# Attention's q and z in pairs of tiles, by seven block products in a stage of their own

## The chip, the core and the metric

The kernel runs on one core of a Trainium2 chip. The metric is the device time of one execution in microseconds; three runs of the kernel before took 3054.83 to 3066.11 us, median 3056.27. PE is the matrix engine (TensorE), DVE VectorE, ACT ScalarE, POOL GpSimd and SP SyncE, which here issues most DMAs.

## What is computed

One layer of a hybrid encoder, for 512 prompt and 64 sample tokens (T = 576) of width 2048:

```python
h = rmsnorm(x, norm_w) * (1.0 + scale[:, None]) + shift[:, None]
proj = h @ w_in          # q|k|v and z, beta, a of DeltaNet; q, k, v, z of attention; indexer; two gates
o_a = gated_delta_rule(l2norm(qa), l2norm(ka), va, g, beta, S0)        # after conv4 and silu
y_a = (rmsnorm(o_a, gdn_norm_w) * silu(z_a)) @ w_branch_a
o_b = sparse_attention(q_b, q_i, w_i, q_pos, K, V, KI, topk, rel_bias) # top-k keys by the indexer's score
y_b = (o_b * jax.nn.silu(z_b)) @ w_branch_b
merged = jax.nn.sigmoid(gl_a) * y_a + jax.nn.sigmoid(gl_b) * y_b
x = x + gate[:, None] * (merged @ w_out)
```

All is fp32. Attention has 16 heads of 128 over two groups of keys and values, DeltaNet 16 heads of 128.

## The kernel before

The projections are a stream of tiles (`plan`). A tile is 128 columns of a weight matrix, all 2048 rows in 16 blocks, times all 576 tokens in two halves of 288. Activations and weights are split into a high part (rounded fp32r) and a low part, and three products are summed (high x high, high x low, low x high), so a tile is 16 x 3 x 2 = 96 matmuls of 288 columns. `load` fetches the raw tile on SP's queue three tiles ahead; `split` makes its parts while the tile before runs: two ACT copies for each of four quarters, and an accumulating DMA from POOL's queue that turns the negated high part into the low part. Each tile ends in an epilogue (`..._epi`) that reads PSUM, and may begin with a `pre`.

All else (indexer scores, top-k, DeltaNet, attention, the ada-gate sums, loads of later stages) is written as generator tasks. After every matmul `tick` (L156) steps the tasks that are due by a cost model of the engines; so the order of all instructions is fixed at build time. `join` (L165) holds the stream until tasks are done and lets tasks alone be issued meanwhile; `drain` joins all tasks. Tiles have few buffers, and `wait`, `take` and `room` make a task wait for their users.

The order of the stream before: k (2 tiles), misc (indexer key, beta, a), 8 indexer q tiles, v (2), a gate tile, `open_gdn` (L1763, drains all but top-k), 6 gate tiles, 16 DeltaNet heads (three conv tiles, then a z tile or gate tile, a few more gate tiles), 3 gate tiles, `open_att` (L1775, drains), 16 pairs of a q and a z tile with 2 gate tiles, 4 z tiles of DeltaNet, `open_ga` (L1786, drains), 8 gate tiles beside `load_ga` (L1558), `open_branch` (drains), then the w_branch_a, w_branch_b and w_out tiles, 16 each.

Attention: `bias_setup` (L1278) writes each head's bias row 128 times to DRAM (3 MB, d_F) at `open_att`. `kv_load` (L1319) fetches a group's keys and values. Per head `qb_epi` copies q out of PSUM and `zb_epi` (L1477) makes silu(z) and spawns `attend` (L1340): it loads the bias tile BT, then four prompt blocks (`attend_block`), each with one logit buffer L; after an odd head `attend_sample` (L1393) does the sample tokens of the pair of heads and stores gb to d_gb. The pres join earlier heads, since qT has two buffers, gb three and zt four. `gate_vectors` (L1510) sums the ada gate on DVE from 64 loads of 256 KB, with a gap of 5000 between them. DeltaNet's `decays` and `solve` of head h wait for the scan of head h-2; `solve` stores N to DRAM (dN), and loads its solved blocks back (TT, Df).

Of the kernel before, what the change touches and what calls it, by code (L numbers as in the profile page):

```python
# [16 lines left out]
D = 2048  # L17
KO = 16
# [190 lines left out]
class Kern(Plan):  # L209
# [53 lines left out]

    def load(self, n):
        if n >= len(self.stream):
            return
        d = self.stream[n]
        m = d["m"] = sum(w for _, _, w in d["srcs"])
        raw = d["raw"] = self.wp.tile([128, 2048], F32, tag="wraw", name=f"wraw{n}")
        r3 = raw[:, :KO * m].rearrange("p (k m) -> p k m", m=m)  # L270
        at = 0
        for src, c, w in d["srcs"]:
            self.S.dma_start(r3[:, :, at:at + w], src[:, c:c + w].rearrange("(k p) m -> p k m", p=128))
            at += w

    def split(self, n, q, of=4, eng=None):
        if n >= len(self.stream):
            return
        d = self.stream[n]
        if q == 0:  # L280
            d["hi"] = self.wp.tile([128, 2048], F32R, tag="whi", name=f"whi{n}")
            d["lo"] = self.wp.tile([128, 2048], F32R, tag="wlo", name=f"wlo{n}")
        w = KO * d["m"] // of
        s = slice(w * q, w * q + w)
        self.A.activation(d["hi"][:, s], d["raw"][:, s], AF.Copy)
        if eng:
            eng.tensor_tensor(d["lo"][:, s], d["raw"][:, s], d["hi"][:, s].bitcast(F32), op=ALU.subtract)
            return

        self.A.activation(d["lo"][:, s], d["hi"][:, s].bitcast(F32), AF.Copy, scale=-1.0)  # L290
        if q % 2:
            s = slice(w * q - w, w * q + w)
            self.G.dma_start(d["lo"][:, s], d["raw"][:, s], accum_op=ALU.add)

    def half(self, n, s, ps, ks, hook=None, part=None):
# [3 lines left out]
        hi = d["hi"][:, :KO * m].rearrange("p (k m) -> p k m", m=m)  # L299
        lo = d["lo"][:, :KO * m].rearrange("p (k m) -> p k m", m=m)  # L300
# [3 lines left out]
        for k in ks:  # L304
            for j, (w, x) in enumerate(((hi, ah), (hi, al), (lo, ah))):
                if part is not None and part != j // 2:
                    continue
                self.mm(ps[:m, :288], w[:, k, :], x[:, k, sl], start=k == 0 and j == 0, stop=k == KO - 1 and j == 2)
# [5 lines left out]
    def run_tile(self, n):  # L314
# [6 lines left out]
        def hook(_):  # L321
            i = count[0] = count[0] + 1
            if i in (4, 14, 24, 34):
                self.split(n + 1, (i - 4) // 10)
            if i == 84:
                self.load(n + 3)

# [19 lines left out]

    def consts(self, ctx):
# [4 lines left out]
        self.mE = cp.tile([128, 2, 128], F32, name="mE")  # L353
# [8 lines left out]
        self.d_g = dt([16, TX], F32, name="d_g")  # L362
        self.d_kT = dt([2, 128, T], F32, name="d_kT")
        self.d_v = dt([T, 256], F32, name="d_v")
        self.d_oa = dt([H, 128, T], F32, name="d_oa")
        self.d_za = dt([H, 128, T], F32, name="d_za")
        self.d_gb = dt([H, 128, T], F32, name="d_gb")
        self.d_t = dt([2, KO, 128, T], F32, name="d_t")
        self.d_ya = dt([KO, 128, T], F32, name="d_ya")
        self.d_F = dt([16, 128, 384], F32, name="d_F")  # L370
# [72 lines left out]
    def start(self, ctx, hctx):  # L443
# [9 lines left out]
        with tc.tile_pool(name="x0", bufs=2, side="right", reuse_waits="tile") as xp:  # L453
# [24 lines left out]
            S.dma_start(self.mE, i["k_mask"])  # L478
# [179 lines left out]
    def misc(self):  # L658
# [3 lines left out]

        for a, b, at in ((0, TP, 0), (TP, T, TP + PAST)):
            c = slice(at, at + b - a)
            A.activation(self.kih[0:64, c], mT[0:64, a:b], AF.Copy)
            A.activation(self.kih[64:128, c], mT[0:64, a:b], AF.Copy)
            for x, R in enumerate((slice(0, 64), slice(64, 128))):
                V.tensor_tensor(self.kil[R, c] if at else self.kiz[R, x, :], mT[0:64, a:b], self.kih[0:64, c].bitcast(F32), op=ALU.subtract)
# [80 lines left out]

    def cache_idx(self):  # L750
# [5 lines left out]
        yield [c]  # L756
# [65 lines left out]
    def score(self, m, qi, qs):  # L822
# [4 lines left out]
        else:  # L827
            yield from self.wait(self.misc_task, self.cache_task)
# [449 lines left out]
    def bias_setup(self):  # L1278

        i, p, V, S = self.i, self.p3, self.V, self.S  # L1280
        oh = p.tile([32, 512], F32, tag="L3", name="oh", bufs=1)
# [3 lines left out]
        self.far = p.tile([128, 16], F32, name="far", bufs=1)  # L1285
        S.dma_start(self.far, i["rel_bias"][15:16, :].partition_broadcast(128).rearrange("p a b -> p (a b)"))
        yield [oh, rb, self.far], 9000
        ps = yield from self.tr("biasp")
        self.mm(ps[:16, :], rb, oh)
        f = p.tile([16, 512], F32, tag="PT3", name="bf", bufs=1)  # L1290
        V.tensor_copy(f, ps[:16, :])
        self.fars = p.tile([128, 8], F32, name="fars", bufs=1)
        v = self.far.rearrange("p (a b) -> p a b", b=2)
# [4 lines left out]
        S.dma_start(self.d_F, f[:, 0:384].unsqueeze(1).to_broadcast([16, 128, 384]))  # L1298
        yield [self.d_F]
# [40 lines left out]
    def attend(self, a):  # L1340
        S, p, h = self.S, self.p3, a["h"]
        yield from self.wait(self.kv_task, self.bias_task)
# [99 lines left out]
    def qb_pre(self, h):  # L1442
        def pre():
# [7 lines left out]
            if h >= 4:  # L1451
                self.join(self.att[(h - 4) | 1]["task"])
                self.join(self.att[(h - 4) | 1]["sample"])
        return pre

    def qb_epi(self, h):
        def epi(ps, s):
            A, V, p = self.A, self.V, self.p3
            if s == 0:
                a = self.att[h] = dict(h=h)  # L1460
# [475 lines left out]
```

## Time and profile before

| | us |
|---|---|
| runs, median (lowest to highest) | 3056.27 (3054.83 to 3066.11) |
| the profiled execution | 3063.92 |
| its span | 3061.8 |
| PE busy | 2934.6 (96%) |
| ACT, DVE, POOL busy | 1533.3, 1204.6, 391.5 |

The profile is of one execution. Busy times are shares of its span; a busy PE is not PE at its peak. Queries on the trace group instructions, list them in time, or follow the chain of waits that ended last.

### The profile page before, as it was taken

The numbers are of one execution on the slowest core, as the hardware profiler recorded it, in microseconds if no ns is written. First come the engines' busy times: TensorE is split into PE (matmuls) and PEld (weight loads), VectorE is DVE, ScalarE is ACT, GpSimd is POOL, SyncE is SP. The second block draws the span as 40 slices with busy tenths as digits, with TensorE's granted clock in tenths as the row PEclk, the third lists the DMA queues.
The fourth block names the chain that finished last, engine by engine and source line by source line (L and its number), as shares of the span: only waits on it lengthen the run. The fifth ranks groups of instructions, "written<-read, shape, count | busy, mean of one in ns | idle before, by whom it ended". The sixth has DMA issues, their size and how long they took to land.

```text
span 3061.8 us, 59253 instructions
## 1 busy us (share of the span) xinstructions
PE 2934.6 (96%) x23931; PEld 2814.4 (92%) x23931; DVE 1204.6 (39%) x3643; ACT 1533.3 (50%) x3428; POOL 391.5 (13%) x776
## 2 busy tenths in 40 slices
PE   6999999999999999999997899999999999999897
PEld 2599999999999999999996899899999899999897
DVE  3344996545455545545531444244412111111112
ACT  3266444556555565555552455355445444444454
POOL 1011111111111111111110001111011111111110
PEclk7999999999999999999998999999999999999999
DMA  9875877677677766676678776777769998888875
GB/s 330 272 160 128 198 184 182 157 163 161 160 163 161 164 159 153 151 172 153 156 160 172 167 169 166 182 169 169 167 152 255 236 232 220 208 215 214 222 160 141
DMA packets 572387, 558.81 MB, mean 183 GB/s; under 512 B 54865, under 2 KB 467426, under 8 KB 570898
## 3 DMA queue, kind: packets, MB, share of 16 engines
q1 hardware_dynamic: 517826, 357.81, 41.3%
q0 software_dynamic: 54144, 197.16, 34.0%
q8 instruction: 188, 3.08, 0.4%
q14 instruction: 85, 0.70, 0.1%
q10 hardware_dynamic: 144, 0.07, 0.0%
HBM read 310.37 MB, written 47.45 MB: 117 GB/s over the span
## 4 chain that ended last, share of the span: by engine, by line
PE 82%; DMA 9%; DVE 3%; ACT 3%; SPq 2%; issue 1%; POOL 0%; ACTq 0%; DVEq 0%; POOLq 0%
PE mm L221 67%; SPq L58 2%; DMA za<-d_za 1%; DMA wlo<-wraw 1%; PE ada L221 1%; PE ob L221 1%; DMA gbl<-d_gb 1%; PE lg L221 1%; PE mmp L221 1%; PE dot L221 1%; PE po L221 1%; DMA xf<-in_x_sample 1%; DMA wa<-in_w_ada 1%; ACT whi L58 1%; ACT wlo L58 1%
## 5 line engine op out<-in xcount | busy, mean ns | idle before, releaser
L221 PE MATMUL mm<-hh,whi 128*128 128x288 f32 (+1 forms) x4448 | 1217.2, 300 | 4.8 <-ACT gth L58 4.5
L221 PE MATMUL mm<-hl,whi 128*128 128x288 f32 (+1 forms) x4448 | 1215.9, 300 | 0.0
L221 PEld LDWEIGHTS mm<-hh,whi 128*128 128x128 f32 (+1 forms) x4448 | 837.8, 188 | 14.0 <-ACT gth L58 5.3
L221 PEld LDWEIGHTS mm<-hl,whi 128*128 128x128 f32 (+1 forms) x4448 | 837.8, 188 | 7.9 <-issue 3.8
L221 PE MATMUL mm<-hh,wlo 128*128 128x288 f32 (+1 forms) x4448 | 683.0, 302 | 4.5 <-DMA wlo<-wraw 4.5
L221 PEld LDWEIGHTS mm<-hh,wlo 128*128 128x128 f32 (+1 forms) x4448 | 615.6, 190 | 6.6 <-DMA wlo<-wraw 4.7
L58 POOL DMA_DIRECT2D wlo<-wraw x376 | 324.0, 862 | 2313.2 <-ACT wlo L58 1926.8
L58 ACT ACTIVATE whi<-wraw 128x512 fp32r<-128x512 f32 x756 | 467.4, 619 | 98.1 <-DMA wraw<-in_w_branch_b 63.1
L58 ACT ACTIVATE wlo<-whi 128x512 fp32r<-128x512 f32 x752 | 475.2, 632 | 76.4 <-PE mm L221 35.9
L221 PE MATMUL mm<-ga,whi 128*128 128x288 f32 x1024 | 142.4, 299 | 7.5 <-DVE ta L58 7.5
L221 PEld LDWEIGHTS mm<-ga,whi 128*128 128x128 f32 x1024 | 139.7, 192 | 8.4 <-DVE ta L58 8.4
L221 PE MATMUL mm<-mg,whi 128*128 128x288 f32 x1024 | 143.6, 297 | 0.0
L221 PE MATMUL mm<-gb,whi 128*128 128x288 f32 x1024 | 138.8, 296 | 0.3 <-DVE tb L58 0.3
L221 PEld LDWEIGHTS mm<-mg,whi 128*128 128x128 f32 x1024 | 138.2, 189 | 0.0
L221 PEld LDWEIGHTS mm<-gb,whi 128*128 128x128 f32 x1024 | 136.8, 188 | 0.6 <-DVE tb L58 0.5
L58 DVE SCALAR_TENSOR_TENSOR cv<-raw,cw,cv 128x579 f32<-128x579 f32 x144 | 117.8, 818 | 33.6 <-ACT cv L58 30.4
L58 DVE SCALAR_TENSOR_TENSOR gacc<-gada,cs,gacc 128x512 f32<-128x512 f32 x120 | 86.7, 744 | 30.9 <-DMA gada<-in_w_ada 30.8
L58 ACT ACTIVATE raw<-mm 128x288 f32<-128x288 f32 x96 | 36.8, 383 | 87.4 <-PE mm L221 86.6
L58 ACT ACTIVATE gth<-mm 128x288 f32<-128x288 f32 x64 | 25.9, 407 | 108.3 <-PE mm L221 104.6
L58 ACT ACTIVATE x<-px 128x128 f32<-128x128 f32 x80 | 22.0, 275 | 116.0 <-PE px L221 115.6
L58 DVE TENSOR_TENSOR xf<-yp,xf 128x512 f32<-128x512 f32 (+1 forms) x18 | 11.4, 632 | 160.5 <-PE yp L236 133.7
L58 DVE SCALAR_TENSOR_TENSOR tb<-tb,mm 128x288 f32<-128x288 f32 x32 | 14.5, 452 | 143.3 <-DMA tb<-d_t 110.3
(493 smaller groups left out, 3422.8 us busy)
## 6 DMA issues: line engine op xcount, KB each, us to landing
wlo<-wraw POOLq DMA_DIRECT2D x376, 512.0 KB, 5.5
wraw<-in_w_in SPq DMA_DIRECT2D x140, 1024.0 KB
wa<-in_w_ada SPq DMA_DIRECT2D x64, 512.0 KB
gada<-in_w_ada SPq DMA_DIRECT2D x64, 256.0 KB
wraw<-in_w_branch_a SPq DMA_DIRECT2D x16, 1024.0 KB
wraw<-in_w_branch_b SPq DMA_DIRECT2D x16, 1024.0 KB
wraw<-in_w_out SPq DMA_DIRECT2D x16, 1024.0 KB
d_t<-gth SPq DMA_DIRECT2D x32, 288.0 KB
```

What stands on the lines that cost most here:

```text
L58: r = f(*a, **k)
L221: self.nc.tensor.matmul(out, lhsT, rhs, start=start, stop=stop, **k)
```

## The change

Attention's q and z tiles leave the stream. Two neighbouring heads' tiles form a pair: weights in blocks A(i,j) (i the head, j the half of the 2048 rows), activations in blocks of row half and token half. Seven products of 128x1024 by 1024x288 replace eight (Winograd's form of Strassen's scheme); each is 8 x 3 = 24 matmuls. The sums of activation blocks are made once (`tblocks`, while four gate tiles run), the sums of weight blocks per pair on DVE (`prep`), which here also makes the low parts; the seven results are combined on DVE out of PSUM. q and silu(z) are stored to DRAM (d_qb, d_zb) from POOL's queue. The stage stands after k, misc, v and 6 gate tiles; the indexer q tiles, scores and top-k come after it, then one gate tile, `open_gdn`, 2 gate tiles and DeltaNet, without the gate tile after every fourth head. In attention the stream holds the 4 left z tiles of DeltaNet and 8 gate tiles, and a task, `heads_in`, loads q and z of each head; 4 gate tiles stand beside `load_ga`. The bias rows are written to DRAM head by head during the pairs, the gap of the ada gate is 2500, and raw, high and low tiles are kept in halves of 1024.

```diff
+    def tblocks(self):
+        for k in range(8):
+            u = {}
+            for n, (kk, t) in enumerate(((k, 0), (k, 1), (k + 8, 0), (k + 8, 1))):
+                u[n] = self.ts.tile([128, 288], F32, tag="s" + "abcd"[n], name=f"u{k}{n}")
+                sl = slice(288 * t, 288 * t + 288)
+                V.tensor_tensor(u[n], f(hh[:, kk, sl]), f(hl[:, kk, sl]), op=ALU.add)
+            yield 300
+            t = {5: u[0], 7: u[1], 6: u[3], 4: u[2]}
+            V.tensor_tensor(t[5], u[1], u[0], op=ALU.subtract)
+            V.tensor_tensor(t[7], u[3], u[1], op=ALU.subtract)
+            V.tensor_tensor(t[6], u[3], t[5], op=ALU.subtract)
+            V.tensor_tensor(t[4], u[2], t[6], op=ALU.subtract)
+            yield ("dve", 300)
+            for x in (5, 7, 6, 4):
+                A.activation(self.TB[x][0][:, k, :], t[x], AF.Copy)
+            yield ("act", 300)
+            for x in (5, 7, 6, 4):
+                V.tensor_tensor(self.TB[x][1][:, k, :], t[x], f(self.TB[x][0][:, k, :]), op=ALU.subtract)
+            yield ("dve", 600)
...
+    def parts(self, p, x, src):
+        d = self.pairs[p]
+        d["hi"][x], d["lo"][x] = hi, lo = [self.wblock("w" + y, f"p{y}{p}{x}", F32R) for y in ("hi", "lo")]
+        for q in range(2):
+            s = slice(512 * q, 512 * q + 512)
+            self.A.activation(hi[:, s], src[:, s], AF.Copy)
+        for q in range(2):
+            s = slice(512 * q, 512 * q + 512)
+            self.V.tensor_tensor(lo[:, s], src[:, s], hi[:, s].bitcast(F32), op=ALU.subtract)
...
+        if step == "A":
+            self.parts(p, 1, a[0, 0])
+            tt(a[1, 0], a[1, 0], a[1, 1], ALU.add)
+        elif step == "B":
+            tt(a[0, 0], a[1, 0], a[0, 0], ALU.subtract)
+            self.parts(p, 6, a[0, 0])
+        elif step == "C":
+            self.parts(p, 5, a[1, 0])
+            tt(a[1, 0], a[0, 1], a[0, 0], ALU.subtract)
+        elif step == "D":
+            self.parts(p, 4, a[1, 1])
+            tt(a[1, 1], a[1, 1], a[0, 0], ALU.subtract)
+            self.pair_load(p + 1, (1, 1))
+        elif step == "E":
+            self.parts(p, 7, a[1, 1])
...
+    def run_pair(self, p, last):
...
+        order = (1, 6, 5, 4, 7, 2, 3)
+        nxt = {x: (p + n // 5, "CDEFGAB"[n]) for n, x in enumerate(order)}
+        for x in order:
...
+            for k in range(8):
+                for j, (w, y) in enumerate(((hi, bh), (hi, bl), (lo, bh))):
+                    self.mm(o, w[:, k, :], y[:, k, :], start=k == 0 and j == 0, stop=k == 7 and j == 2)
+                    i += 1
+                    if i == 2 and self.posts:
+                        self.posts.pop(0)()
+                    if i == 4:
+                        self.prep(*nxt[x])
...
+    def heads_in(self):
+        p, S = self.p3, self.S
+        for h in range(H):
             if h % 8 == 0:
                 if h:
-                    self.join(self.att[h - 1]["task"])
-                    self.join(self.att[h - 1]["sample"])
+                    yield from self.wait(self.att[h - 1]["task"])
+                    yield from self.wait(self.att[h - 1]["sample"])
                 self.kv_task = self.spawn(self.kv_load(h // 8))
             if h >= 2:
-                self.join(self.att[h - 2]["task"])
...
+                yield from self.wait(self.att[h - 2]["task"])
+            for d in (3, 4):
+                if h >= d:
+                    t = self.att[(h - d) | 1]
+                    if t["h"] < h - 1 or d == 4:
+                        yield from self.wait(t["task"])
+                        yield from self.wait(t["sample"])
+            a = dict(h=h)
...
+            S.dma_start(a["qT"], self.d_qb[h][:, :TP])
...
+            S.dma_start(a["zt"], self.d_zb[h])
...
+            a["task"] = self.spawn(self.attend(a))
+            yield 1000
...
-        gate(6, self.open_gdn)
+        gate(2, self.open_gdn)
...
-            if h % 4 == 3:
-                gate(1)
         gate(3)
-        for h in range(H):
-            self.win(f"qb{h}", O_QB + 128 * h, self.qb_epi(h), self.open_att if h == 0 else self.qb_pre(h))
-            self.win(f"zb{h}", O_ZB + 128 * h, self.zb_epi(h))
-            if h == 7:
-                gate(2)
-        z(len(zs))
-        gate(len(gates), self.open_ga)
+        left = [z] * len(zs) + [gate] * (len(gates) - 4)
...
+        gate(4, self.open_ga)
...
-            self.topk_gap, self.solve_gap, self.gada_gap = 100, 0, 5000
+            self.topk_gap, self.solve_gap, self.gada_gap = 100, 0, 2500
```

## Rows read from the trace of the kernel before

**Rows 1.** The page, part 1: busy time, share of the span, instructions.
```profile
PE 2934.6 (96%) x23931; PEld 2814.4 (92%) x23931; DVE 1204.6 (39%) x3643; ACT 1533.3 (50%) x3428; POOL 391.5 (13%) x776
```

**Rows 2.** Chain of waits, 300 to 560 us: start, duration, what.
```profile
325.70 114.50 PE mm L221 x864
```

**Rows 3.** Windows: stretch, length, busy by engine, granted clock, DMA share, GB/s.
```profile
550.00:1600.00 1050.00, 1033.80 (x9991) 1005.48 (x9990) 518.03 (x1924) 613.74 (x1490) 161.05 (x468) 1.00 0.70 160
1650.00:1700.00 50.00, 26.40 (x166) 24.63 (x165) 6.80 (x23) 7.98 (x17) 1.90 (x3) 0.76 0.92 160
1600.00:2300.00 700.00, 660.61 (x4787) 631.97 (x4786) 241.47 (x723) 322.77 (x682) 68.86 (x80) 0.97 0.73 169
2350.00:2450.00 100.00, 92.05 (x668) 91.12 (x667) 20.63 (x44) 46.37 (x90) 12.04 (x14) 0.97 0.95 241
```

**Rows 4.** Groups of instructions, shapes apart: busy us, mean ns | idle before, releaser.
```profile
L58 ACT ACTIVATE whi<-wraw 128x512 fp32r<-128x512 f32 x752 | 465.4, 619 | 95.7 <-DMA wraw<-in_w_branch_b 63.1 <-PE mm L221 13.5 <-DMA wraw<-in_w_in 9.5
L58 DVE TENSOR_TENSOR tb<-tb,yl 128x288 f32<-128x288 f32 x32 | 14.7, 458 | 8.0 <-DMA yl<-d_ya 7.0
L58 DVE TENSOR_TENSOR xf<-yp,xf 128x512 f32<-128x512 f32 x14 | 9.7, 692 | 147.2 <-PE yp L236 120.3 <-DMA xf<-in_x_prompt 26.8
```

**Rows 5.** Top-k's instructions by tile: ns min/median/max, first and last start.
```profile
L58 DVE MAX8 max8p<-msk x48: 387/561/697, 312.0 to 372.6; 128x8 f32<-128x256 f32 x16, 128x8 f32<-128x384 f32 x16, 128x8 f32<-128x512 f32 x16
L58 DVE MATCH_REPLACE8 msks<-max8s,msks x32: 1266/1268/1271, 375.9 to 498.8; 64x1088 f32<-64x1088 f32 x32
```

**Rows 6.** Timeline of SP's queue in DeltaNet: start, issue time, what.
```profile
413.62 1.85 SPq L58 DMA_DIRECT2D gB<-d_g  x1
...
447.24 0.34 SPq L58 DMA_DIRECT2D dN<-e  x1
...
510.45 0.42 SPq L58 DMA_DIRECT2D Df<-d_D  x1
...
597.50 0.33 SPq L58 DMA_DIRECT2D dN<-e  x1
...
622.13 0.37 SPq L58 DMA_DIRECT2D Df<-d_D  x1
...
921.65 0.32 SPq L58 DMA_DIRECT2D d_oa<-oT  x1
...
1053.11 0.32 SPq L58 DMA_DIRECT2D d_oa<-oT  x1
```

**Rows 7.** Timeline of SP's queue in attention.
```profile
1782.16 1.83 SPq L58 DMA_DIRECT2D BT<-d_F  x1
...
1824.38 0.80 SPq L58 DMA_DIRECT2D d_gb<-gb  x2
...
1962.35 0.41 SPq L58 DMA_DIRECT2D KT<-d_kT  x1
...
2069.02 0.90 SPq L58 DMA_DIRECT2D d_gb<-gb  x2
...
2205.92 0.90 SPq L58 DMA_DIRECT2D d_gb<-gb  x2
```

**Rows 8.** Timeline of DVE in attention.
```profile
1801.71 0.29 DVE L58 SCALAR_TENSOR_TENSOR gb<-ob,zt 128x128 f32<-128x128 f32 x1 [0.20 <-PE ob L221]
...
1984.77 0.69 DVE L58 COPY KC<-kcp 128x512 f32<-128x512 f32 x1 [1.14 <-PE kcp L236]
```

**Rows 9.** Chain of waits in attention, its opening and one head.
```profile
1649.32 24.92 DMA wlo<-wraw
...
1689.90 4.36 DMA BT<-d_F
...
1789.16 1.50 PE lg L221 x4
```

**Rows 10.** Timeline of SP's queue, loads of the DeltaNet output, first and last of 32.
```profile
2297.06 0.42 SPq L58 DMA_DIRECT2D oa<-d_oa  x1
...
2389.40 0.32 SPq L58 DMA_DIRECT2D oa<-d_oa  x1
```

More of the change, by code (lines that the diff above doesn't have):

```diff
@@ L262, in win, with wblock @@
         self.add(name, [(self.i["w_in"][0], c, n)], lambda: self.h, epi, pre)
+    def wblock(self, kind, name, r=F32):
+        return self.wp.tile([128, 1024], r, tag=kind, name=name, bufs=4)
     def load(self, n):
-        if n >= len(self.stream):
+        if n >= min(len(self.stream), self.edge):
             return
@@ L268, in load @@
         m = d["m"] = sum(w for _, _, w in d["srcs"])
[L269 to L274, printed above, removed]
+        d["raw"] = []
+        for b in range(2):
+            raw = self.wblock("wraw", f"wraw{n}_{b}")
+            d["raw"].append(raw)
+            r3 = raw[:, :8 * m].rearrange("p (k m) -> p k m", m=m)
+            at = 0
+            for src, c, w in d["srcs"]:
+                self.S.dma_start(r3[:, :, at:at + w], src[1024 * b:1024 * b + 1024, c:c + w].rearrange("(k p) m -> p k m", p=128))
+                at += w
     def split(self, n, q, of=4, eng=None):
-        if n >= len(self.stream):
+        if n >= min(len(self.stream), self.edge):
             return
@@ new lines, in pair_load @@
+    def pair_load(self, p, which):
+        if p >= len(self.pairs):
+            return
+        i, j = which
+        n = self.nraw = self.nraw + 1
+        t = (self.ts.tile([128, 1024], F32, tag="wx", name=f"wx{p}{i}{j}") if n % 5 == 0 else self.wblock("wraw", f"wp{p}{i}{j}"))
+        c = self.pairs[p]["col"] + 128 * i
+        self.S.dma_start(t.rearrange("p (k m) -> p k m", m=128),
+                         self.i["w_in"][0][1024 * j:1024 * j + 1024, c:c + 128].rearrange("(k p) m -> p k m", p=128))
+        self.pairs[p]["A"][i, j] = t
@@ new lines, in pair_out @@
+    def pair_out(self, p, which, x, done):
+        A, V, ts, d = self.A, self.V, self.ts, self.pairs[p]
+        i, t = which
+        kind, h = d["to"][i]
+        dst = (self.d_qb if kind == "q" else self.d_zb)[h][:, 288 * t:288 * t + 288]
+        if kind == "z":
+            e = ts.tile([128, 288], F32, tag="se", name=f"e{p}{i}{t}")
+            A.activation(e, x, AF.Tanh, scale=0.5)
+            V.scalar_tensor_tensor(done, e, 1.0, x, op0=ALU.add, op1=ALU.mult)
+        return self.spawn(self.store(dst, done, self.G))
@@ new lines, in run_pairs, with last @@
+    def run_pairs(self, after):
+        def last(x):
+            if x == 7:
+                self.edge = 1 << 30
+                self.load(after)
+                self.load(after + 1)
+            elif x in (2, 3):
+                for q in ((0, 1) if x == 2 else (2, 3)):
+                    self.split(after, q)
+        self.posts = []
+        self.join(self.tb_task)
+        self.room(self.ts, 1)
+        self.pair_load(1, (0, 0))
+        for p in range(len(self.pairs)):
+            self.run_pair(p, last if p == len(self.pairs) - 1 else None)
+        for f in self.posts:
+            f()
+        self.load(after + 2)
+        self.drain()
+        self.cts.close()
+        self.ctb.close()
@@ L827, in score @@
         else:
-            yield from self.wait(self.misc_task, self.cache_task)
+            yield from self.wait(self.keys_task, self.cache_task)
         units = []
@@ L1341, in attend @@
         S, p, h = self.S, self.p3, a["h"]
-        yield from self.wait(self.kv_task, self.bias_task)
+        yield from self.wait(self.kv_task)
         BT = p.tile([128, 256], F32, tag="BT", name=f"BT{h}")
@@ L1726, in z @@
                 self.win(f"za{h}", O_ZA + 128 * h, self.za_epi(h))
+        gate(2)
+        gate(4, self.open_pairs)
+        self.edge = self.nA = len(self.stream)
+        self.pairs = [dict(col=o + 128 * h, to=((k, h), (k, h + 1)), A={}, hi={}, lo={})
+                      for h in range(0, H, 2) for k, o in (("q", O_QB), ("z", O_ZB))]
+        for m in range(8):
+            self.win(f"qi{m}", O_QI + 128 * m, self.qi_epi(m), self.open_idx if m == 0 else None)
         gate(1)
-        gate(6, self.open_gdn)
+        gate(2, self.open_gdn)
         for h in range(H):
@@ L1869, in run @@
             self.load(4)
-            for n in range(2, len(self.stream) - 2):
+            for n in range(2, self.nA):
+                self.run_tile(n)
+            self.run_pairs(self.nA)
+            for n in range(self.nA, len(self.stream) - 2):
                 self.run_tile(n)
```

260 lines of the change are left out of this document (170 added, 90 removed).

## The prediction

> **What bounds the kernel now.** I read the page's busy times first. TensorE (PE) is busy 2934.6 of 3061.8 us [rows 1]: it idles only 127 us, and no other engine is busy for more than half of the span. Nearly all of the PE time is one kind of matmul, 128x128 weights on 288 columns. The chain of waits prices it where nothing interrupts: 864 of them in 114.50 us, 132.5 ns each [rows 2], so a tile of 96 costs 12.72 us. Then I asked for windows, to see where the 127 us lie. The whole DeltaNet stage, 550 to 1600, has PE busy 1033.8 of 1050; attention with its opening, 1600 to 2300, 660.6 of 700, so 39.4 us idle, most of it in the opening; the two windows around the loading of the DeltaNet output, 2350 to 2450, lack 8.0 [rows 3]. So a removed matmul is worth its full price only if the stages that lose their cover of matmuls do not begin to wait. That is what I price below.
>
> **Part 1, the products.** A pair of tiles cost 2 x 96 = 192 matmuls and costs 7 x 24 = 168. 16 pairs, 24 fewer each, 384 x 132.5 ns = **-50.9 us**. The weight load per matmul stays.
>
> **Part 2, the stage of pairs itself.** A pair is 168 x 132.5 = 22.3 us of PE. Per pair VectorE gets 14 low parts of 512 columns, four sums of 1024, seven sums of 288 out of PSUM, and for z four more of 288. With 692 ns for 512 columns, twice that for 1024 and 458 for 288 [rows 4] this is 9.7 + 5.5 + 3.2 = 18.4 us for q, 20.2 for z: under 22.3, but close. ScalarE has 14 copies of 619 ns plus tanh, about 10 us. The one-off sums of the activations are 96 VectorE operations of 458 ns, 44 us, beside four gate tiles, 50.9. Loads fall from 1 MB per 12.7 us to 2 MB per 22.3, the accumulating DMA goes from these tiles, and the stores and the bias rows are on POOL's queue, where nothing waits for them at once. What remains is filling and refilling: bounds 0 and 15 us, I take **+5**; if the cover on VectorE is gone the price is in rival C.
>
> **Part 3, top-k moves next to DeltaNet.** Top-k is VectorE work from 312.0 to 498.8; the first DeltaNet transfer (gB) is issued at 413.62, 102 us after its start [rows 5, 6]. Afterwards only two tiles, 25 us, stand between them, so some 75 us more of top-k lie on DeltaNet heads that already use half of VectorE (518.0 of 1050) [rows 3]. What such an overlap does is seen in head 0: from storing N to loading its solved blocks took 63.2 us (447.24 to 510.45), in head 2 without top-k 24.6 (597.50 to 622.13) [rows 6]. So bounds 0 and 39 us; with all of it behind the tiles that follow head 0 (three gate tiles more than later heads have) much is covered: I take **+8**.
>
> **Part 4, four gate tiles leave DeltaNet.** If they only filled waits, all 51 us come back as idle time; if the stage is bound by PE, nothing. Two heads of four tiles each took 131.4 us between output stores (921.65 to 1053.11) [rows 6], while PE idled 16.2 us in the whole 1050 [rows 3]. Near the second end: **+4**.
>
> **Part 5, attention loses its cover.** Before, its stage held 32 q and z tiles and 6 others. Now it holds 4 z and 8 gate tiles: 12 x 12.72 = 153 us. Attention's own PE work is what two pairs of heads took beyond their eight tiles: 2069.02 to 2205.92 is 136.9, less 101.8, so 17.5 per pair, 140 in all [rows 7]. PE content: 293 us. The chain is longer. `heads_in` lets odd head h start only when the sample part of the pair before it is done (the three gb buffers), and that sample part starts only when its odd head is done: pairs run one after the other. One such cycle is in the trace: bias tile issued 1782.16, first logits 1789.16 (7.0), last prompt block 1802.00 (12.8), sample stored 1824.38 (22.4): 42.2 us [rows 7 to 9]. Loading a group's keys and values took 1962.35 to 1985.5, 23.1 [rows 7, 8].
> First pair: 23.1 + 7.0 + 12.8, about 10 for the second head, which waits for the first one's logit buffers, and 22.4 = 75.3. Three more cycles: 202. By then PE has spent 70 on attention and 132 on tiles; 21 us of tiles are left and run under the second group's loading. After that nothing but attention is issued until `open_ga` has drained it. Second group, again 75.3: 277. Three cycles without tiles: the logits after the issue, and each step behind stream matmuls, get shorter; I estimate 36 (between 31, the steps of [rows 7 to 9] without the matmuls between them, and 42): 385. Idle 385 - 293 = 92, against 39.4 before [rows 3]: **+53**. The bounds: openings of 60 and 55 with cycles of 36 and 31 give 316, idle 23, so -16; openings of 80 with cycles of 45 and 42 give 421, idle 128, so +89. The 3 MB write of the bias rows, behind which the queue stood before (the chain waits 24.92 us there for an accumulating DMA [rows 9]), is gone from the opening; that gain is inside the 39.4. The ada-gate sums (gap now 2500) take 64 x about 4.5 = 290 us of the order, shorter than the chain.
> The clock in the emptiest window, 1650 to 1700, with PE busy 26.4 of 50 us after that DMA wait, was 0.76 of full speed, a mix of the levels of 1.2 and 2.4 GHz; in the fuller 2350 to 2450 it was 0.97 [rows 3, 9]. I add nothing for it; the upper bound holds it. The Trainium skill ("TensorE: Matmul & The Clock Gate", Part 1) says that the slower clock is the default and that sustained activity releases the faster one; the trace agrees in direction. By that rule the four uncovered pairs would run 70 us of PE work at half rate, about half of it on the chain, and the sum would end 35 us later.
> The transfer in each cycle is 4.36 us in the chain of waits (BT) [rows 9]. The Trainium skill ("DMA: Bandwidth & Descriptors", Anatomy of one DMA) gives about 2 us fixed plus bytes over 436 GB/s, an estimate of 2.3 us for these 128 KB. By it the eight cycles would be 16 us shorter; the row decides.
>
> **Part 6, the last gates.** Loading the DeltaNet output (32 steps) ran from 2297.06 to past 2389.40, 2.97 us a step, beside eight gate tiles and a DMA share of 0.95 [rows 3, 10]. Four tiles, 50.9 us, now cover 17 steps. The other 15, with no weights beside them, cost between 1.0 and 2.97 us each, 15 to 45; I take 1.8: 27, less the 8.0 idle before: **+19** (7 to 37).
>
> **Sum.** -50.9 + 5 + 8 + 4 + 53 + 19 = +38. The profiled execution took 3063.92, 2.1 more than its span and 7.65 more than the median of 3056.27. So 3102 against it, and **3094 us** against the median; this case's own range is 3060 to 3130 (attention's term alone between +20 and +85).
>
> **Rivals.**
> *A, faster.* Attention's cycles are short enough that the 12 tiles nearly cover them. The other terms sum to -15, so it decides where attention's term is below +15: idle below 55, stage below 348, a mean cycle near 36 with tiles and 31 without. For it: much of the 42.2 us is planned order behind stream matmuls, and even heads run beside the samples. Against: the cycle is dependent steps on four engines, and SP issues the next loads only behind the sample's store. With an attention term of 0, +10 for part 6 and half the other costs: 3056 - 51 + 0 + 10 + 9 = about 3024 to 3030.
> *B, DeltaNet's chain becomes the bound.* Top-k stretches two heads by up to 39 and half of the four gates comes back as waiting, 25: 64 instead of the 12 taken, 3146. For: the decay of head h waits for the scan of head h-2. Against: 131.4 us for two heads with PE full.
> *C, the pairs do not run at PE's rate.* If VectorE waits for ScalarE's high part at each of the seven products (0.62) and at four tanh (taken at 458 ns, as the operation behind it), z pairs take 20.2 + 4.3 + 1.8 = 26.3 and q pairs 22.7: 2.2 us per pair on average over 22.3, +35, so 3129. The saving is then nearly all lost. Against: the sources of all but one of the products are ready a product earlier.
>
> **Chances.** Forecast 0.54, A 0.25, B 0.11, C 0.10. What this kernel's measurement can tell from no change is about 0.5%, 15 us: the forecast's own spread leaves some of it within that. Faster by more 0.24, within 0.16, slower 0.60. Range 3020 to 3150: it takes in A and most of B and C.
>
> **What will show it.** Part 1: the stage of pairs lasts 16 x 22.3 = 357 us with PE full; if longer, rival C, and VectorE will be late. Part 5: from the opening of attention to its last sample store 385 us, PE busy near 9 tenths while tiles last, then 4 to 6 tenths over some 160 us with a clock below 1; sample stores 42 us apart, then 36. If PE stays full there, the prediction is wrong and A holds. Part 6: PE idle for some 27 us before the first w_branch_a tile. Parts 3 and 4: DeltaNet heads 67 us apart, the first two slower; PE idle of more than 30 us in that stage means B.

## The result and the profile after

The changed kernel takes 3132.02 us (median; 3129.55 to 3134.10) against 3060.28 for the kernel before on the same chip: ratio 1.0238, 95% interval [1.0220, 1.0256]. The forecast was 3094: the sign is right, but the loss is 72 us where 38 were forecast. The profiled execution has a span of 3130.9, 69.1 more than before.

First the page after: busy times, and of the 40 slices the rows of PE and of its granted clock.

```profile
PE 2947.4 (94%) x23547; PEld 2803.0 (90%) x23547; DVE 1491.1 (48%) x4123; ACT 1514.5 (48%) x3412; POOL 380.4 (12%) x792
...
PE   6999999999999999999999999899666799999997
...
PEclk8999999999999999999999999999867899999999
```

The 384 matmuls are gone (23931 before), yet PE is busy 12.8 us longer than in [rows 1]. The last two rows say where to look: slices 29 to 32, some 2190 to 2505, are six or seven tenths busy at a clock of 0.6 to 0.8. The windows of the kernel after (columns as in [rows 3]: PE, weight loads, DVE, ACT, POOL, clock, DMA share) show the stages beside them:

```profile
300.00:590.00 290.00, 289.85 (x2167) 288.46 (x2165) 220.05 (x348) 112.91 (x218) 34.30 (x64) 1.00 0.50 129
800.00:1950.00 1150.00, 1137.87 (x10892) 1109.35 (x10892) 690.81 (x2304) 663.72 (x1585) 181.21 (x526) 1.00 0.72 161
2000.00:2200.00 200.00, 193.77 (x1364) 180.34 (x1363) 101.94 (x317) 102.37 (x234) 16.39 (x19) 0.98 0.76 194
2250.00:2400.00 150.00, 92.92 (x379) 65.46 (x379) 84.84 (x270) 46.73 (x120) 0.00 (x0) 0.73 0.25 79
2430.00:2510.00 80.00, 62.68 (x412) 59.09 (x411) 26.55 (x59) 38.20 (x76) 8.22 (x10) 0.83 0.87 226
```

The pairs run with PE full, DeltaNet nearly so. The stretch 2250 to 2400, after the last tile of attention's stage, is the bad one, then the load of the DeltaNet output. SP's queue in the kernel after gives the milestones (start, issue time, transfer):

```profile
1971.76 0.38 SPq L58 DMA_DIRECT2D d_t<-gth  x1
...
1980.57 0.64 SPq L58 DMA_DIRECT2D KT<-d_kT  x1
...
2067.81 0.80 SPq L58 DMA_DIRECT2D d_gb<-gb  x2
...
2117.46 0.82 SPq L58 DMA_DIRECT2D d_gb<-gb  x2
...
2167.83 0.80 SPq L58 DMA_DIRECT2D d_gb<-gb  x2
...
2214.27 0.80 SPq L58 DMA_DIRECT2D d_gb<-gb  x2
...
2281.57 0.80 SPq L58 DMA_DIRECT2D d_gb<-gb  x2
...
2327.93 0.80 SPq L58 DMA_DIRECT2D d_gb<-gb  x2
...
2372.38 0.80 SPq L58 DMA_DIRECT2D d_gb<-gb  x2
...
2409.41 0.80 SPq L58 DMA_DIRECT2D d_gb<-gb  x2
2410.26 0.46 SPq L58 DMA_DIRECT2D oa<-d_oa  x1
```

Attention's stage opens at 1971.76 (the last gate store ahead of it; 1619.76 before) and ends with the first load of the DeltaNet output at 2410.26 (2297.06 before, [rows 10]): 438.5 us, eight pairs of heads, each closed by its sample store. With these milestones and the first DeltaNet transfer (413.62 before, [rows 6], 814.42 after) the two executions can be set against each other. Tiles that a stretch gained or lost are taken out at 12.72 us, a pair of tiles at 7 x 24 x 132.5 ns = 22.26.

| stretch | before | after | of that, tiles | rest | forecast |
|---|---|---|---|---|---|
| start to first DeltaNet transfer | 413.6 | 814.4 | +16 pairs, +2 tiles: +381.6 | +19.2 | +5 (part 2) |
| DeltaNet to the opening of attention | 1206.1 | 1157.3 | -4: -50.9 | +2.1 | +12 (parts 3, 4) |
| attention's stage | 677.3 | 438.5 | -26: -330.7 | +91.9 | +53 (part 5) |
| load of the DeltaNet output, to the end of w_branch_a | 321.9 | 286.2 | -4: -50.9 | +15.2 | +19 (part 6) |
| from there to the end | 442.8 | 434.4 | 0 | -8.4 | 0 |

The rests add to +120.0; with the products' -50.9 that is the 69.1. Part 5 alone is 39 above its forecast, and above its upper bound of 89.

### The profile page after: what moved, and what is told of

Same layout as the page of the kernel before. It is cut to its first block, busy times and chain, and to the rows that moved or that the text cites. A ratio compares the mean times of both kernels' runs of the same rounds, so it can differ in the third digit from the quotient of the medians.

```text
span 3130.9 us, 59965 instructions
## 1 busy us (share of the span) xinstructions
PE 2947.4 (94%) x23547; PEld 2803.0 (90%) x23547; DVE 1491.1 (48%) x4123; ACT 1514.5 (48%) x3412; POOL 380.4 (12%) x792
## 4 chain that ended last, share of the span: by engine, by line
PE 84%; DMA 6%; DVE 5%; ACT 2%; issue 1%; SPq 1%; POOL 0%; ACTq 0%; DVEq 0%; POOLq 0%
PE mm L221 58%; PE P L221 11%; PE ob L221 1%; DMA za<-d_za 1%; PE lg L221 1%; PE ada L221 1%; PE mmp L221 1%; PE po L221 1%; PE dot L221 1%; PE obs L221 1%; DMA xf<-in_x_sample 1%; DMA wa<-in_w_ada 1%; DVE L L58 1%; DMA kst<-in_cache_k 1%; PE u L221 1%
## 5 line engine op out<-in xcount | busy, mean ns | idle before, releaser
L221 PE MATMUL mm<-hh,whi 128*128 128x288 f32 (+1 forms) x3424 | 949.8, 303 | 6.5 <-DVE qi L58 6.5
L221 PE MATMUL mm<-hl,whi 128*128 128x288 f32 (+1 forms) x3424 | 942.8, 300 | 0.0
L221 PEld LDWEIGHTS mm<-hh,whi 128*128 128x128 f32 (+1 forms) x3424 | 648.3, 189 | 11.7 <-issue 9.4
L221 PEld LDWEIGHTS mm<-hl,whi 128*128 128x128 f32 (+1 forms) x3424 | 648.1, 189 | 3.0 <-issue 0.7
L221 PE MATMUL mm<-hh,wlo 128*128 128x288 f32 (+1 forms) x3424 | 528.9, 302 | 0.0
L221 PEld LDWEIGHTS mm<-hh,wlo 128*128 128x128 f32 (+1 forms) x3424 | 473.9, 189 | 3.7 <-issue 0.2
L58 ACT ACTIVATE whi<-wraw 128x512 fp32r<-128x512 f32 (+1 forms) x628 | 388.5, 619 | 51.6 <-PE mm L221 41.0
L221 PE MATMUL mm<-ga,whi 128*128 128x288 f32 x1024 | 146.5, 302 | 17.3 <-ACT ga L58 17.3
L221 PEld LDWEIGHTS mm<-ga,whi 128*128 128x128 f32 x1024 | 141.2, 192 | 20.9 <-ACT ga L58 19.5
L58 DVE SCALAR_TENSOR_TENSOR cv<-raw,cw,cv 128x579 f32<-128x579 f32 x144 | 118.1, 820 | 33.4 <-ACT cv L58 30.1
L58 DVE TENSOR_TENSOR plo<-wp,phi 128x512 fp32r<-128x512 f32 x182 | 116.5, 686 | 16.1 <-ACT phi L58 15.3
L221 PE MATMUL P<-hh,plo 128*128 128x288 f32 x384 | 113.7, 296 | 0.0
L221 PE MATMUL P<-hl,phi 128*128 128x288 f32 x384 | 113.5, 296 | 0.0
```

Of the source, the lines that this page charges most:

```text
L58: r = f(*a, **k)
L221: self.nc.tensor.matmul(out, lhsT, rhs, start=start, stop=stop, **k)
```

## The experiments

Times are medians, each with the kernel before (3060 to 3063) on the same chip. "Stage" runs from the issue of the first KT to the first load of the DeltaNet output; the spacings are those between sample stores: three in the first group, the second group's opening, three in the second group. "Tail" is what passes between the last sample store and the first load. Stage, spacings and tail are of the profiled execution.

| kernel | edit | us | ratio to before, 95% | stage | spacings | tail |
|---|---|---|---|---|---|---|
| changed | none | 3132.0 | 1.0238 [1.0220, 1.0256] | 429.7 | 49.7 50.4 46.4, 67.3, 46.4 44.5 37.0 | 1 |
| e1 | four gb buffers | 3077.8 | 1.0051 [1.0034, 1.0068] | 377.5 | 29.5 39.8 25.9, 90.7, 26.6 28.0 21.4 | 30 |
| e2 | PE kept active | 3111.9 | 1.0162 [1.0139, 1.0185] | 414.4 | 51.0 50.4 46.4, 64.5, 45.7 39.8 35.8 | 1 |
| e3 | plain tiles | 3166.4 | 1.0335 [1.0314, 1.0356] | 432.2 | 52.5 50.4 46.4, 67.3, 46.5 44.8 37.1 | 1 |
| e4 | ada gate left out | 3095.5 | 1.0105 [1.0088, 1.0122] | 411.7 | 47.2 49.0 48.4, 69.9, 41.0 41.0 33.7 | 1 |
| e5 | e1, denser ada gate | 3080.6 | 1.0064 [1.0046, 1.0082] | 381.8 | 34.0 40.7 27.6, 96.6, 23.9 38.5 20.3 | 18 |
| e7 | e5, keys and values loaded in two tasks | 3082.4 | 1.0066 [1.0050, 1.0082] | 379.1 | 28.4 40.4 26.1, 65.9, 52.6 24.0 33.5 | 23 |
| e8 | e7 with e2's matmuls | 3073.1 | 1.0037 [1.0026, 1.0048] | 373.6 | 28.4 40.4 26.1, 69.3, 50.3 20.9 29.9 | 23 |
| e9 | e7, ada loads on POOL's queue | 3081.8 | 1.0066 [1.0042, 1.0090] | 366.0 | 28.4 40.4 26.1, 72.3, 53.8 25.0 33.4 | 1 |
| e10 | changed, ada loads on POOL's queue | 3126.8 | 1.0218 [1.0198, 1.0239] | 431.7 | 51.3 50.4 47.7, 67.4, 46.3 45.8 36.5 | 1 |
| e11 | e7, ada gate left out | 3021.2 | 0.9870 [0.9850, 0.9889] | 331.1 | 31.2 36.9 22.4, 70.8, 45.6 25.2 22.2 | 1 |
| e14 | e7, ada gate spread | 3052.9 | 0.9967 [0.9955, 0.9980] | 333.0 | 27.6 38.0 31.3, 83.8, 27.2 27.7 17.6 | 1 |
| e15 | e14, sums on POOL | 3070.5 | 1.0031 [1.0019, 1.0043] | 350.1 | 33.9 39.1 28.7, 68.5, 47.2 22.7 26.4 | 1 |
| e16 | e14, moved parts earlier | 3040.5 | 0.9934 [0.9917, 0.9950] | 334.7 | 27.6 38.0 31.3, 83.7, 27.3 27.5 19.0 | 2 |
| e17 | e16 with e2's matmuls | 3038.1 | 0.9922 [0.9907, 0.9937] | 333.0 | 28.2 38.1 31.3, 83.7, 27.1 27.4 18.1 | 1 |

**e1, four gb buffers.**

```diff
-            for d in (3, 4):
+            for d in (4,):
...
-            a["gb"] = p.tile([128, T], F32, tag="gb", name=f"gb{h}", bufs=3)
+            a["gb"] = p.tile([128, T], F32, tag="gb", name=f"gb{h}", bufs=4)
```

> Attention's gb gets four buffers instead of three and the wait that went with three is dropped, so an odd head no longer waits for the sample part of the pair before it; only a pair waits for the sample part two pairs back. Theory S (the pairs of heads run one after the other, and that serial cycle is what made attention long): sample stores 30 to 38 us apart instead of 44 to 50, attention from its opening to the first load of the DeltaNet output 330 to 370 us instead of 438, the whole 3035 to 3070. Theory K (the slow matrix clock of the stretch without tiles is what made it long): the first group, where the clock was 0.97, keeps its 46 to 50 us, the whole within 15 us of 3132.

54 us come back. The spacings fall to 21 to 40 us, in the covered first group too, where the clock had been 0.98: pairs ran one after the other, and that made the stage long. Only the second group's opening grew, from 67.3 to 90.7 us, likely because its first two pairs now run beside each other: with the spacing behind it, it takes 117.3, 4 us more than in the changed kernel. The stage from its opening is 386 us, 16 above S's range, and the whole misses S's by 8, for a reason that neither theory held. SP's queue in e1:

```profile
2274.89 0.80 SPq L58 DMA_DIRECT2D d_gb<-gb  x2
2302.87 0.80 SPq L58 DMA_DIRECT2D d_gb<-gb  x2
...
2324.28 0.80 SPq L58 DMA_DIRECT2D d_gb<-gb  x2
2325.73 28.92 SPq L58 DMA_DIRECT2D gada<-in_w_ada  x13
2354.70 0.42 SPq L58 DMA_DIRECT2D oa<-d_oa  x1
```

All heads are done at 2324; then come 13 pieces of the ada gate, 29 us of loads and VectorE sums with nothing beside them. The background task is now what ends last.

**e2, keeping PE active.** In place of the drain at the end of attention:

```diff
+        while self.tasks:
+            due = min(t.due for t in self.tasks)
+            if due > self.pe:
+                idle += due - self.pe
+                self.pe = due
+            if idle > 300:
...
+                self.mm(ps[:, :288], self.h[0][:, 0, 0:128], self.h[0][:, 0, 0:288])
+                idle, n = 0.0, n + 1
+            self.tick()
```

> While the stream of tiles is held at the end of attention, a 288-column matmul whose result nobody reads is issued after every 0.3 us or more of planned idle time, so that the matrix engine stays active; it is added work and changes no output. Theory K (slow clock): the granted clock of 2200 to 2400 rises from 0.73 to 0.95 or more, the uncovered cycles shrink from 44 to about 36 us and the second group's opening from 67 to about 60, the whole 3090 to 3105. Theory S (serial cycle): the covered cycles took 46 to 50 us at a clock of 0.97, longer than the uncovered ones, so a faster clock gives at most 10 us, and the added matmuls in front of the chain may cost as much: 3122 to 3150.

213 matmuls more and 20 us less, between the two theories. Windows of e2, which the stretch 2250:2400 of the kernel after answers to:

```profile
2250.00:2300.00 50.00, 36.27 (x203) 28.19 (x201) 31.02 (x103) 18.30 (x46) 0.00 (x0) 0.93 0.27 85
2300.00:2350.00 50.00, 39.25 (x191) 31.30 (x191) 27.59 (x87) 15.20 (x39) 0.00 (x0) 0.80 0.27 86
```

The clock rises from 0.73 to 0.80 to 0.93. From the second KT to the first load it is 184.2 us (193.5 before the edit), and the load that follows takes 75.7 instead of 82.2 to the first gate of w_branch_a: 15.8 us stand where the clock rose. The profiled executions are 26.8 us apart; the other 11 are there at the third sample store already (2167.83, in e2 2156.4), ahead of the first added matmul (2200.37), and aren't the edit's. So the slow clock is real, and raising it this far is worth some 16 us, not most of the loss. What it does to the chain is seen in the kernel after, the same matmuls in a covered stretch and in the bare one:

```profile
2138.78 1.72 PE L221 MATMUL ob<-PT,V 128*128 128x128 f32 x14
...
2342.51 3.28 PE L221 MATMUL ob<-PT,V 128*128 128x128 f32 x14
```

**e3, the order without the seven products.** The stage of pairs holds 32 plain tiles:

```diff
+        for h in range(H):
+            for k, o in (("q", O_QB), ("z", O_ZB)):
+                self.win(f"{k}b{h}", o + 128 * h, self.qz_epi(k, h))
...
-            self.run_pairs(self.nA)
```

> The stage of pairs is kept in its place, with its stores through DRAM, but its tiles are ordinary ones: 32 tiles of 96 matmuls, low parts by the accumulating DMA, no sums of blocks. All else is as in the changed kernel. If the seven products give their full price and the stage's overhead of 19 us is what the block sums and refills cost: 50.9 more less 10 to 19, 3164 to 3173; attention's stage stays at 438 within 10. Rival (the stage of pairs loses elsewhere too, in the refilled weights of the indexer's first tiles): 3140 to 3164. If the products had given nothing, 3132 or less.

As expected: 3166 us, and 441 from the opening to the first load. The first DeltaNet transfer, in the kernel after and in e3 (times from first to last):

```profile
L58 SPq DMA_DIRECT2D gB<-d_g x16: 426/433/1187, 814.4 to 1848.6; - x16
```

```profile
L58 SPq DMA_DIRECT2D gB<-d_g x16: 426/434/1128, 850.7 to 1884.1; - x16
```

It comes 36.3 us later with plain tiles; so of the products' 50.9 the block sums and the start of the stage eat 14.6, and 34.4 reach the end. The order by itself (own stage, DRAM, attention without cover) costs 104 against the kernel before.

**e4, no ada gate.**

```diff
-        self.spawn(self.gate_vectors())
+        self.V.memset(self.gate, 0.5)
```

> Leaves out the sums of the ada gate in the attention stage (64 loads of 256 KB and 128 VectorE operations of about 0.7 us, 90 us of VectorE in all); the gate is set to a constant. If these operations stand in the chain of the attention heads (theory V): 3 to 6 us off each cycle, 25 to 50 in all, 3082 to 3107. If they lie beside it (theories S and K): within 12 us of 3132.

The ada gate is left out here. 36.5 us less than the changed kernel, in V's range. From the opening to the first load it is 414.3 instead of 438.5, and the load takes 73.7 instead of 82.2. But the covered spacings stay at 47 to 49: the ada gate is not what made those long.

**e5 and e7, the tail.** e5 is e1 with `gada_gap` 1200. e7 adds this:

```diff
+        self.kc_task = self.spawn(self.kc_load(n, KC))
+        yield [V, KT]
...
+        yield from self.wait(self.kc_task)
         yield from self.take("Ls")
...
-        self.spawn(self.conv_out())
-        self.spawn(self.gate_vectors())
         self.spawn(self.heads_in())
+        self.spawn(self.gate_vectors())
+        self.spawn(self.conv_out())
```

> Four gb buffers as in e1, and the planned gap between the pieces of the ada-gate sums 1200 instead of 2500. In e1 the last sample store was at 2324.3, but 13 pieces of the ada gate were still to do, and the load of the DeltaNet output began at 2354.7. If the tail of e1 was only the planned gap: these 30 us go, the stage of attention 340 to 350 us, the whole 3043 to 3053, below the kernel before (3062). If the pieces (two VectorE operations of about 0.7 us and a load of 256 KB on the same queue as the heads' loads) stand in the chain of the heads: packed twice as dense they give back 10 to 25 us, 3055 to 3075.

> As e5, and the keys and values of a group are loaded in two tasks: the prompt blocks wait for the loads of KT and V alone, only the sample parts wait for the transposed key cache; the heads' first loads are issued ahead of the ada gate's. In e1 the two groups' openings took 85 us (from the issue of KT to the first sample store) and 91 us (from the store before to the store after). Theory O (the opening is the transposes of the key cache, with their two loads, in front of the first logits): 15 to 20 us off each opening, the whole 3005 to 3020. Rival (the opening is the heads' own chain and SP's queue, where loads of the ada gate stand in front): 0 to 10 us off e5, 3035 to 3050.

Both missed: 3080.6 and 3082.4, no better than e1; e7 is 32 us above its rival's range too. A denser ada gate shortened the tail to 18 us and gave it back in the spacings (e5, 6 us above even the second expectation). e7's shorter second opening (65.9) was followed by a spacing of 52.6. The chain of waits of e7 in that stretch (start, length, what) and one row of SP's queue show why there are two candidates:

```profile
2257.95 1.20 DVE Ls L58
2259.19 0.15 DVE sms L58
2259.34 0.33 DVE L L58
2259.67 0.66 DVE gacc L58
2260.33 0.20 DVE gb L58
```

```profile
2242.67 20.72 SPq L58 DMA_DIRECT2D gada<-in_w_ada  x4
2263.44 1.09 SPq L58 DMA_DIRECT2D BTs<-d_F  x2
```

VectorE's piece (gacc) stands in the chain of the heads, and SP stands 20.7 us at loads that wait for a buffer, with the next pair's bias tile behind them. Which one costs?

**e9 and e10, the ada loads on POOL's queue,** in e7 and in the changed kernel:

```diff
-                self.S.dma_start(raws[n], i["w_ada"][0, k:k + 128, col:col + 512])
+                self.G.dma_start(raws[n], i["w_ada"][0, k:k + 128, col:col + 512])
```

> As e7, and the 64 loads of the ada gate are issued from POOL's queue instead of SP's. In e7 SP stood up to 20.7 us at one run of these loads (they wait for a buffer that VectorE has still to read), with the heads' loads behind it; 10 pieces, 23 us, still came after the last sample store. Theory Q (the ada gate costs by blocking SP's queue): 20 to 35 us off e7, 3045 to 3060. Theory V (it costs by its two VectorE operations a piece, which the chain of waits shows between the heads' own): within 8 us of e7, 3075 to 3090.

> The changed kernel with one edit: the loads of the ada gate are issued from POOL's queue. Without the ada gate altogether (e4) it was 36 us faster. Theory Q: most of these 36 come back, 3098 to 3112. Theory V: 0 to 10, 3122 to 3134. The cycles stay serial, 44 to 50 us covered.

0.6 and 5.3 us, in V's ranges: SP's queue was not it, in either kernel. In e9 the stage is 13 us shorter and the tail went to 1 us, but the load after it grew from 85 us to 105. The pieces of the ada gate had moved behind the tail: VectorE still sums them until 2372, and PE stands in front of the matmuls (gsum) that close them, in e9 behind the first load, in e7 (27.5 us) mostly ahead of it. PE's longest wait in e9 between 2346 and 2452 (total, times, longest):

```profile
PE gsum L221 <- DVE gacc L58: 26.7, 1, 26.7
```

**e11, e7 without the ada gate** (edit as in e4):

> As e7 with the sums of the ada gate left out (the gate is a constant): the lower bound of what attention costs when pairs overlap and nothing else uses VectorE or SP's queue. e7 had 23 us of ada gate alone at the end, and e4 against the changed kernel gave 36 with serial pairs. If both costs are the ada gate's and add up: 3025 to 3045. If the overlapping pairs are bound by their own chain or by PE (293 us of PE work, estimated, against 379 from KT to the last load): 3050 to 3062, only the tail gone.

3021, below every expectation: the ada gate costs 61 us in e7. 23 of them are the tail. For the others VectorE's pieces in the heads' chain are the likely cause, since moving the loads' issue (e9, e10) gave nearly nothing; but no run keeps the loads and takes only the sums away, so the loads' traffic isn't ruled out. That the time is 1.3% below the kernel before is not yet a win, as the kernel before does sum its ada gate.

**e8, e7 with the matmuls of e2.**

> As e7, with the unread matmuls of e2 while the stream is held at the end of attention. In e2 they raised the granted clock of the uncovered stretch from 0.73 to 0.80 to 0.93 and took 9 us off that stretch and 6 off the next. With overlapping pairs the uncovered stretch is shorter and already at 0.90 in its first part: theory K gives 3 to 10 us off e7; theory S 0 to 8 us more than e7.

9 us less, within K's range.

**e14 and e16, the ada gate elsewhere.** One group of 16 pieces stands beside k, misc and v, one beside the indexer's tiles, two stay in attention; the last argument is the gap. In e16 the first two gaps are 0 and 500:

```diff
+            self.spawn(self.gate_vectors(self.p1, 0, 1, 1000))
...
+        self.spawn(self.gate_vectors(p, 1, 2, 2000))
...
+        self.spawn(self.gate_vectors(self.p3, 2, 4, 4500))
```

> As e7, with the ada gate's four groups of 16 pieces in other places: one group beside the first tiles (k, misc, v), one beside the indexer's tiles, two in attention with a gap of 4500. Nothing is left out. e7 was 3082 and e11, without the ada gate, 3021: 23 us of the 61 were the tail behind the last sample store, 38 lay inside. Theory V: half the pieces inside cost 19, the tail goes, the two groups moved lie beside full PE work and cost 0 to 10: 3040 to 3050, faster than the kernel before (3060) by 10 to 20. Rival: the moved groups delay the index keys or the scores, and DeltaNet starts 15 to 25 us later: 3055 to 3070.

> As e14, with the planned gaps of the two moved groups 0 and 500 instead of 1000 and 2000, so that their last pieces and sums come before the stage is drained. In e14 the first group's sums held the matrix engine for 13 us before the gate tiles (gap 8.3 behind the last VectorE piece, then the sums), and DeltaNet started 22 us later than in the changed kernel. If that remainder is these waits: 12 to 18 us off e14, 3035 to 3042, below the kernel before (3062) by over 0.5%. If it is the VectorE work itself that delays the index keys and scores: within 5 us of e14, 3048 to 3058.

e14 is 9 us below the kernel before, 3 above the range expected: its stage is 97 us shorter than the changed kernel's, but DeltaNet starts 22 us later. The row of PE where the first group's sums stand, in e14 and then in e16 (the bracket is PE's idle time before them):

```profile
227.64 3.81 PE L221 MATMUL gsum<-ones,gacc 128*128 128x1 f32 x16 [8.09 <-DVE gacc L58]
```

```profile
222.63 3.81 PE L221 MATMUL gsum<-ones,gacc 128*128 128x1 f32 x16 [1.96 <-DVE gacc L58]
```

With the pieces ahead of the drain 6 of the 8 us of waiting go, DeltaNet starts 9 us earlier (827.8 against 836.9), and the whole is 12 us faster: 3040.5, within the first expectation, ratio 0.9934 [0.9917, 0.9950]. Nothing is left out in e16, so this version beats the kernel before by 0.7%, and the changed one by some 3%.

**e15, the attention part of the sums on POOL.** The gap of that part is 3000 instead of 4500, and the tile ncr, through which the conv states go out, has one buffer instead of two.

```diff
+                x = acc[s] if k == 0 else raws[n] if s else p.tile([128, 512], F32, tag="gtmp", name=f"gtmp{n}", bufs=1)
+                self.G.tensor_scalar(x, raws[n], c, None, op0=ALU.mult)
+                if k:
+                    self.G.tensor_tensor(acc[s], acc[s], x, op=ALU.add)
...
-        self.spawn(self.gate_vectors(self.p3, 2, 4, 4500))
+        self.spawn(self.gate_vectors(self.p3, 2, 4, 3000))
```

> As e14, and the two groups in attention are summed on POOL (a product and a sum for each token group, four operations a piece) instead of VectorE. Loads and SP's queue as in e14. Theory V: attention as in e11, 3021 to 3040. Rival (what costs is the loads on SP's queue, or POOL's accumulating transfers for the tiles stand behind the new operations): no better than e14, 3040 to 3065.

18 us slower than e14 and above both expectations. PE does not wait for POOL's accumulating transfers in that stage, so the rival's second reason is out. The buffer of ncr shows: PE stands 16.1 us behind it as the stage opens, but behind ncr and the key cache it stood 12.5 in e14, and the first opening is only 3.3 us longer. The likely reason for the rest, which no run isolates, is in the last section.

**e17, e16 with the matmuls of e2.**

> As e16, with the unread matmuls of e2 while the stream is held at the end of attention. Theory K: the uncovered stretch is now about 60 us long at a clock near 0.93, so 2 to 8 us off e16. Theory S: no change within 4, or up to 6 more for the added matmuls in front of the chain.

2.5 us less than e16, not to be told from it; both theories' ranges hold it. The clock of the bare stretch, some 70 us, did rise, from 0.87 in e16 to 0.93 (2252 to the first load), so little was left for it.

## Why the prediction was right in sign and wrong in size

- Part 1 holds: the products are worth their price. PE is full from 300 to 590, and rival C is out.
- Part 2 was +19 instead of +5. Two waits were not seen. The first pair waits for block sums of the activations that VectorE makes late (the last piece of T6's low part begins at 280.2, its first product at 274.5): its second and third products take 11.7 us (274.50 to 286.23) where 48 matmuls cost 6.4. PE idles only 3.0 us of that; then its matmuls start 240 ns apart instead of 133 for some 3 us (granted clock 0.89 from 275 to 290). And PE stands 6.5 us in the first indexer tile, whose epilogue is behind the index key; that key now returns through DRAM, and ScalarE waits 13.0 us for it. In e3, which has the same order, PE does not wait there; e3 shows 4.6 us of the 19 all the same.

```profile
279.57 0.40 PE L221 MATMUL P<-T6h,phi 128*128 128x288 f32 x1 [2.13 <-ACT T6h L58]
280.69 0.40 PE L221 MATMUL P<-T6l,phi 128*128 128x288 f32 x1 [0.72 <-DVE T6l L58]
...
283.02 0.44 PE L221 MATMUL P<-T5l,phi 128*128 128x288 f32 x1
283.26 0.44 PE L221 MATMUL P<-T5h,plo 128*128 128x288 f32 x1
...
660.33 0.58 PE L221 MATMUL mm<-hh,whi 128*128 128x288 f32 x1 [6.48 <-DVE qi L58]
```

- Parts 3 and 4 were +2 instead of +12. Top-k did stretch the first two heads, as Part 3 said (from storing N to loading its blocks 69.5 and 76.9 us), but nearly all of it was covered; rival B is out.
- **Part 5 is the step that failed.** Its mechanism, attention without cover in a serial chain of pairs, was right: undoing the serial part alone gives back 54 of the 72 us (e1). Its size was not. From opening to first load it forecast 75.3, three cycles of 42.2, 75.3, three of 36: 385. Measured were 96.1, 146.5 for three, 67.3, 127.8 for three, and 0.8: 438.5, which is 53 more. (The table above shows only 39 of these, since attention's own PE work had been taken 14 us too small: 677.3 less 38 tiles and 39.4 idle leaves 154.5, not 140; part of the 14 may be the slower clock of the opening.) Three sentences of it were at fault.

  The first: "The ada-gate sums ... take ... 290 us of the order, shorter than the chain" treated a task that shares VectorE with the chain as lying beside it. Without it the stage is 24 us shorter, and the load after it 8 (e4).

  The second: "I add nothing for it", for the clock. Raising the clock gave 16 (e2). The Trainium skill's rule, which the text had weighed ("TensorE: Matmul & The Clock Gate", Part 1), agrees in direction; the prediction's estimate by that rule was 35.

  The third is the price of a cycle, read from one cycle of the kernel before: with cover and without the ada gate it still took 47 to 49 us, not 42.2, and the first opening 83, not 75 (e4; with the ada gate 96). Here is one cycle of the changed kernel, from the sample store at 2117.46 to the next at 2167.83:

```profile
2119.88 0.47 SPq L58 DMA_DIRECT2D BT<-d_F  x1
...
2128.28 1.66 PE L221 MATMUL lg<-KT,qT 128*128 128x512 f32 x4
...
2140.66 1.67 PE L221 MATMUL lg<-KT,qT 128*128 128x512 f32 x4
...
2143.53 0.39 PE L221 MATMUL ob<-PT,V 128*128 128x128 f32 x2
```

  It is 10.8 us to the first logits, 15.6 to the last prompt block and 23.9 to the store, where 7.0, 12.8 and 22.4 were forecast. The largest part is the start: the forecast began at the issue of BT, but in the changed kernel q and z come from DRAM too, and their loads stand ahead of BT in SP's queue (2.4 us). The even head, whose logits begin at 2140.66, does not stretch the sample part: that took 23.9 us in the third cycle as well, which has no even head. The three sizes come from separate kernels and need not add up.
- Part 6 was +15 against +19, right. The last stretch was 8 us shorter than before: in the kernel before PE stood once for 8.3 us behind ScalarE's tile og early in the w_out stage, in the changed kernel 0.65. Why is open.
- Rival A, the faster outcome, needed a stage below 348 us. The chain alone was too long for it, but its condition was a good one: e14 and e16 meet it (342 and 344 from opening to first load) and are faster than before.
- Two agreements are luck. Outside part 5 the rests sum to 28 where 36 were forecast, because 14 too little in part 2 meet 22 too much elsewhere. And rival C's 3129 is the number nearest to 3132, but PE was full in the stage of pairs.

## What to carry to other kernels

Price the stage that loses its cover by its longest serial chain, and count every background task that shares an engine with it: the ada gate cost 36 us beside the serial chain (e4) and 61 beside the overlapping one (e11). Look for the buffer count that makes units run one after the other; here one more buffer of 2.3 KB per partition was worth more than the 384 matmuls. Saved work and the order needed to save it are best measured apart: here they were -34 and +104.

## What the runs showed of the hardware

VectorE slowed down beside POOL, which e15 did not expect. The same VectorE operations from 2000 to 2350 in e14 and then in e15, where POOL does 124 operations of 512 columns, 1.3 to 1.75 us each, beside them:

```profile
L58 DVE SCALAR_TENSOR_TENSOR L<-lg,BT 128x256 f32<-128x256 f32 x48 | 20.1, 421 | 31.6 <-ACT L L58 30.1 <-PE lg L221 0.5
...
L58 DVE CUSTOM_DVE_ANT_0 L<-L,msk 128x384 f32<-128x384 f32 x16 | 8.8, 550 | 0.0
...
L58 DVE TENSOR_SCALAR L<-L,smp 128x384 f32<-128x384 f32 x16 | 6.7, 420 | 0.6
```

```profile
L58 DVE SCALAR_TENSOR_TENSOR L<-lg,BT 128x256 f32<-128x256 f32 x48 | 20.0, 422 | 40.6 <-ACT L L58 33.4 <-DMA BT<-d_F 5.0 <-PE lg L221 1.4
...
L58 DVE CUSTOM_DVE_ANT_0 L<-L,msk 128x384 f32<-128x384 f32 x16 | 12.1, 754 | 0.0
L58 DVE TENSOR_SCALAR L<-L,smp 128x384 f32<-128x384 f32 x16 | 11.2, 699 | 0.6
```

Two operations that work in SBUF alone went from 550 to 754 ns and from 420 to 699; the one that also reads PSUM stayed at 421. So moving the sums to POOL took VectorE's 745 ns pieces away (44 us) and made the heads' own steps longer: the masks and scalings of L and Ls together by 27 us. In the chain of waits from 2090 on, VectorE's steps on L hold 13.0% in e15 and 4.4% in e14, so these steps are likely what made e15 slower. The Trainium skill says that VectorE and GpSimd share a pair of SBUF ports, which one of them holds to the exclusion of the other ("Trainium Architecture — The Big Picture", What this means for kernel authors); the two rows in SBUF agree in direction.

The clock row is the other one: with PE busy 62% of a stretch in small pieces the granted clock was 0.73, a mix of 1.2 and 2.4 GHz, and 213 matmuls strewn into the gaps brought it to 0.80 to 0.93; some 16 us of the 20 that e2 gained stand there and in the load behind it.
